# A two-layer diffusion block on one core: modulation sums, attention copies, layer 1's projection and its end rearranged

## The chip, the cores and the metric

The kernel runs on one core of one Trainium2 chip. The time is device microseconds of one execution; lower is better. Three runs gave 2876.41, 2872.47 and 2872.45 us, so the median is 2872.47 us.

## The reference

Two layers work on 1024 latent tokens and, in layer 0, on 256 context tokens, 1024 features each, in float32. Six modulation vectors per layer come from the conditions:

```python
m_lat = split(silu(c) @ ada_w[l] + ada_b[l], 6)      # m_ctx from c_ctx
h = x * (1 + m[1]) + m[0]
y = mixer(h)                                         # attention and output projection
x = layer_norm(DN_ALPHA * x + m[2] * y, ln_g[l, 0], ln_b[l, 0])
f = conv_ffn(x * (1 + m[4]) + m[3])                  # up, 3-tap convolution, silu(g) * a, down
x = layer_norm(DN_ALPHA * x + m[5] * f, ln_g[l, 1], ln_b[l, 1])
```

Layer 0's mixer has global attention (8 query heads over 2 key heads, "A") and neighbourhood attention (8 heads, "B"). Layer 1's has a window of 128 tokens to each side ("C"). All latent queries also read the context keys. Only the latent tokens of layer 1 are returned.

## The kernel before

Every large product is three fp32r products of operands split into a rounded part (hi) and the rest (lo). The hi cast is a ScalarE copy, the lo part a subtraction on VectorE or GpSimd. "The order by hand" below means that a region fixes the order of all engines' instructions; elsewhere only TensorE's order is fixed and a scheduler places the others.

**Layer 0's projection (`l0_project`).** `mm` banks of 128 tokens are made in turn with the weights `wq`, `wk`, `wv`, and then feature-wise with `wb` (the query part, `qB`) and `wb2` (the key part, `kB`), 12 evictions each. Beside it, the generator `ada_items` makes the modulation parts 2 to 5 of layer 0: eight chunks of 512 columns, each with four loads `araw` on SP's queue (512 KB), 16 multiply-adds `acc` on VectorE for the two conditions, and for each condition `ada_sum`: a hi/lo split `ahl`, two TensorE products with a matrix of ones into `small`, the bias row `abr`, and a store. `bg(n)` advances it by up to n steps and stops at a `"hold"`. What is left is drained when `kB` is done. The context rows are loaded by `load_x(2)` behind the four `wk` tokens that precede their first use; they wait for a buffer of the pool `xp`.

**Attention A (`groups_a`, `pv2_banks`).** Two key heads (kv), each with two context groups and eight latent groups. A latent group makes context scores, latent scores for two pairs of heads, the softmax, and ten banks of P transposes `T` in PSUM (three buffers), which `evict` copies to `PT`; the product `pv` reads these. `evict` takes VectorE in four of ten cases by a running counter, so the order of the engines within a group depends on where the counter stands.

**Output projection (`out_project`).** For each block of 128 tokens: load `yr`, split it into `yh`, `yl` (GpSimd makes `yl`), 48 products, gate, residual, statistics, normalisation. The block before is then turned by `finish`; in layer 1 this is `build_B1`, which also makes the four difference tiles `tt` of a Strassen-like scheme from block t and block t-4, t = 4 to 7. They go through memory (`T1`) and come back as T0 to T3 in `ffn7`; those of the last block stay in SBUF. Layer 1 takes the blocks in order 0 to 7. `first_x` and `rest` are the first products of layer 1's up projection.

**Layer 1's feed-forward (`ffn7`), in an order by hand.** First the up products and the convolution, with `store` and `mix` for the halves; then the down products in 77 steps of 12 matmuls into the banks `dx` and `dy`, with jobs hung on steps: loads of two steps ahead, `scale` of the residual, `evict` and `end`. `vs` holds a partial sum for the right half. The last nine steps run block by block, so that blocks 4 to 7 are done one after another, each followed by `evict` and `end`, where `finish_o` writes the output.

## Time and profile before

| what | value |
|---|---|
| median of three runs | 2872.47 us |
| profiled execution, its own time | 2874.48 us |
| its span | 2872.6 us |
| TensorE busy | 2747.7 us, 96% |
| VectorE / ScalarE / GpSimd busy | 2145.0 / 1388.0 / 667.2 us |
| chain that ended last | PE 70%, DVE 9%, issue 9%, DMA 5%, ACT 4%, POOL 2% |

PE is TensorE, PEld its weight loads, DVE VectorE, ACT ScalarE, POOL GpSimd, SP SyncE. In a timeline a row has start, duration, engine, line, operation, output and inputs, shape and count; in brackets stands the idle time of the engine before it and what ended it. In a table by windows the columns are the stretch, its length, busy time and count of PE, PEld, DVE, ACT and POOL, then the granted TensorE clock, the DMA share and GB/s.

### The profile page before, as it was taken

The numbers are of one execution on the slowest core, as the hardware profiler recorded it, in microseconds if no ns is written. First come the engines' busy times: TensorE is split into PE (matmuls) and PEld (weight loads), VectorE is DVE, ScalarE is ACT, GpSimd is POOL, SyncE is SP. The second block draws the span as 40 slices with busy tenths as digits, with TensorE's granted clock in tenths as the row PEclk, the third lists the DMA queues.
The fourth block names the chain that finished last, engine by engine and source line by source line (L and its number), as shares of the span: only waits on it lengthen the run. The fifth ranks groups of instructions, "written<-read, shape, count | busy, mean of one in ns | idle before, by whom it ended". The sixth has DMA issues, their size and how long they took to land.

```text
span 2872.6 us, 45400 instructions
## 1 busy us (share of the span) xinstructions
PE 2747.7 (96%) x16724; PEld 2244.9 (78%) x16724; DVE 2145.0 (75%) x3852; ACT 1388.0 (48%) x2607; POOL 667.2 (23%) x948
## 2 busy tenths in 40 slices
PE   8999799899999999999999999999998999999997
PEld 6787577777789988888888888766677788888886
DVE  4765676667588777888878656677778888888778
ACT  4321255567435655455553344167743555445541
POOL 4501243354451000000001002255644011111002
PEclk9999899999999999999999999999999999999998
DMA  7568611032558753333458525652244355555962
GB/s 272 153 206 279 214 32 43 9 134 92 169 161 243 216 165 108 110 114 110 121 197 294 173 98 171 199 165 81 83 132 162 120 180 176 165 173 205 329 218 90
DMA packets 369222, 457.02 MB, mean 159 GB/s; under 512 B 26008, under 2 KB 265016, under 8 KB 367464
## 3 DMA queue, kind: packets, MB, share of 16 engines
q1 hardware_dynamic: 341512, 369.53, 40.5%
q0 software_dynamic: 24592, 82.89, 8.3%
q8 instruction: 131, 2.15, 0.3%
q10 hardware_dynamic: 2896, 1.70, 0.2%
q14 instruction: 91, 0.75, 0.1%
HBM read 338.11 MB, written 115.93 MB: 158 GB/s over the span
## 4 chain that ended last, share of the span: by engine, by line
PE 70%; DVE 9%; issue 9%; DMA 5%; ACT 4%; POOL 2%; SPq 0%; ACTq 0%; POOLq 0%; DVEq 0%
PE q L1842 8%; PE x L1842 7%; PE y L1842 7%; PE S L882 4%; PE v L1842 4%; PE pv L1027 3%; PE mm L405 3%; PE mm L407 3%; PE mm L406 3%; PE T L1013 3%; PE dy L2524 3%; PE d L407 3%; PE d L406 3%; PE d L405 3%; PE dx L2524 2%
## 5 line engine op out<-in xcount | busy, mean ns | idle before, releaser
L906 POOL TENSOR_SCALAR P<-P,rin 128x640 f32<-128x640 f32 (+3 forms) x288 | 253.0, 882 | 333.8 <-DVE rin L905 301.8
L1816 DVE TENSOR_TENSOR w<-raw,w 128x512 fp32r<-128x512 f32 x308 | 208.6, 691 | 90.1 <-ACT w L1814 89.9
L113 DVE TENSOR_TENSOR w<-raw,w 128x512 fp32r<-128x512 f32 x315 | 204.5, 689 | 86.4 <-ACT w L112 83.1
L112 ACT CAST w<-raw 128x512 fp32r<-128x512 f32 x315 | 183.4, 620 | 173.4 <-PE d L407 67.2
L882 PE MATMUL S<-k,q 64*128 64x256 f32 (+2 forms) x1824 | 194.9, 337 | 17.3 <-DVE nm L2862 8.3
L903 ACT ACTIVATE P<-P,nm 128x641 f32<-128x641 f32 (+4 forms) x208 | 161.5, 778 | 84.9 <-DVE nm L2862 43.9
L1814 ACT CAST w<-raw 128x512 fp32r<-128x512 f32 x308 | 182.3, 620 | 15.1 <-DVE raw L1821 9.9
L882 PEld LDWEIGHTS S<-k,q 64*128 64x128 f32 x1824 | 136.9, 187 | 54.5 <-issue 19.1
L893 ACT COPY PT<-T 128x512 f32<-128x512 f32 (+1 forms) x250 | 134.9, 566 | 82.7 <-PE T L1013 80.0
L1027 PE MATMUL pv<-PT,v 128*64 128x128 f32 x2016 | 132.9, 279 | 16.6 <-ACT PT L893 13.9
L1013 PE MATMUL T<-ident,P 128*128 128x128 f32 x1008 | 135.8, 282 | 9.5 <-POOL P L906 3.3
L1027 PEld LDWEIGHTS pv<-PT,v 128*64 128x64 f32 x2016 | 108.5, 137 | 42.7 <-ACT PT L893 23.2
L405 PE MATMUL d<-w,w 128*128 128x512 f32 x352 | 137.5, 391 | 0.0
L407 PE MATMUL d<-w,w 128*128 128x512 f32 x352 | 137.0, 389 | 0.0
L406 PE MATMUL d<-w,w 128*128 128x512 f32 x352 | 137.0, 389 | 0.0
L1013 PEld LDWEIGHTS T<-ident,P 128*128 128x128 f32 x1008 | 110.4, 142 | 29.8 <-issue 17.4
L891 DVE COPY PT<-T 128x512 f32<-128x512 f32 (+1 forms) x166 | 110.4, 666 | 31.0 <-PE T L1013 21.1
L905 DVE RECIPROCAL rin<-den 128x1 f32<-128x1 f32 x288 | 46.0, 161 | 112.1 <-ACT P L903 108.7
L1842 PE MATMUL q<-T3h,w 128*128 128x512 f32 x352 | 121.1, 405 | 7.6 <-DVE ug L2479 4.0
L2524 PE MATMUL dy<-w,w 128*128 128x512 f32 x528 | 120.7, 390 | 0.0
L1842 PE MATMUL q<-T2h,w 128*128 128x512 f32 x352 | 115.9, 390 | 2.3 <-ACT q L2461 1.8
L903 ACT ACTIVATE P<-P,mc 128x1280 f32<-128x1280 f32 (+1 forms) x80 | 94.7, 1186 | 46.0 <-DVE mc L1148 41.6
(450 smaller groups left out, 7779.6 us busy)
## 6 DMA issues: line engine op xcount, KB each, us to landing
raw<-in_up_dram SPq DMA_DIRECT2D x132, 512.0 KB
raw<-in_down_dram SPq DMA_DIRECT2D x59, 512.0 KB
raw<-g SPq DMA_DIRECT2D x44, 512.0 KB
raw<-G SPq DMA_DIRECT2D x38, 512.0 KB
araw<-in_ada_w_dram SPq DMA_DIRECT2D x32, 512.0 KB
raw<-in_w_in_dram SPq DMA_DIRECT2D x28, 512.0 KB
g<-cv POOLq DMA_DIRECT2D x22, 512.0 KB, 3.0
G<-go POOLq DMA_DIRECT2D x44, 256.0 KB, 2.7
```

What stands on the lines that cost most here:

```text
L113: (lo_eng or nc.vector).tensor_sub(lo, s, f32(hi))
L405: nc.tensor.matmul(ps, lh, rh, start=first, stop=False)
L406: nc.tensor.matmul(ps, lh, rl, start=False, stop=False)
L407: nc.tensor.matmul(ps, ll, rh, start=False, stop=last)
L882: self.nc.tensor.matmul(outs[a], q[r, x, qs], k[r, y, ks], start=(i == 0), stop=(i == 2))
L903: nc.scalar.activation(P[:, :m], P[:, :m], AF.Exp, bias=negm, scale=-1.0, accum_out=den)
L906: nc.gpsimd.tensor_scalar(P[:, :n], P[:, :n], rin, 1.0, ALU.mult, ALU.mult)
L1013: nc.tensor.transpose(ps[:, s * 128 : (s + 1) * 128], P[a][:, cols[i + x] : cols[i + x] + 128], self.ident,)
L1027: nc.tensor.matmul(O[a * HD : (a + 1) * HD], v_of(a, vts[i + x]), pT[:, s * 128 : (s + 1) * 128], start=(i + x == 0), stop=(i + x == m - 1 ...
L1816: nc.vector.tensor_sub(half(i, 1), src[i], f32(half(i, 0)))
L1842: nc.tensor.matmul(ps, w[:, a, s], r[b][:, k], start=first and k + i == 0, stop=k == 3 and i == 2, skip_group_check=True,)
L2524: nc.tensor.matmul(banks[q][t], ga[i][:, a, c], wd[i][:, b], start=q < 2 and f + k == 0, stop=f == HF - 1 and k == 2, skip_group_check=True,)
```

## The change

1. Layer 0's projection. The context rows are loaded into the pool `raw` at the end of the first stage. The modulation is no longer advanced beside `wq` and `wk`. A sum's products stand in a list, `pend`, and are issued three visits or more after their split (or when the next chunk's first split comes); no hold ends a visit. `split`, `abr` and the bias loads are arranged per chunk.
2. Attention A. The ten `PT` copies of a latent group get named engines: `DDADA` and `AADDA` (D VectorE, A ScalarE).
3. Output projections. `yr` is loaded into `yl` and split in place.
4. Layer 1's end. Blocks in the order 0, 4, 1, 5, 2, 6, 3, 7; blocks 0 to 3 leave their float32 tiles as `b`, so `tt` takes four subtractions in place of six; the lo subtraction goes from GpSimd to VectorE; the last block's second half is scaled on VectorE; four weight parts move from `rest` to `first_x`; the Silu table is loaded in `rest`.
5. `ffn7`. One addition moves from `store` to `mix`; two more buffers in a new pool and one more in `fgs`, loads reach up to one pair further ahead; `vs` is gated and added to `z` in jobs of their own (`gated`, `shared`), so `evict` has three instructions and not four; `scale` earlier; the Sqrt table is loaded at step 67.
6. The last block's normalisation (`last_o`): Sqrt on ScalarE, a reciprocal, one Newton-like correction in five small ScalarE instructions, and the output in two halves on two queues.

The diff, cut:

```diff
@@ ada_items @@
-                        yield from self.ada_sum(tp, bank, acc[v], l, v, part, o, W)
-                yield
+                        if v == vecs[0]:
+                            while self.pend:
+                                self.pend.pop(0)[1]()
+                            br = self.t(tp, [64, W], "abr")
...
+                        self.ada_late(tp, bank, acc[v], br[i : i + 1], l, v, part, o, W, i)
+                        yield
@@ new: ada_late @@
+        hl = self.t(tp, [128, 2, W], "ahl", R, bufs=2)
+        nc.scalar.copy(hl[:, 0], acc)
+        nc.vector.tensor_sub(hl[:, 1], acc, f32(hl[:, 0]))
+        def late():
+            ps = bank()
+            nc.tensor.matmul(ps[:, :W], self.ones, hl[:, 0], start=True, stop=False)
+            nc.tensor.matmul(ps[:, :W], self.ones, hl[:, 1], start=False, stop=True)
+            nc.vector.tensor_add(br, ps[i : i + 1, :W], br)
+            nc.sync.dma_start(self.d["ada"][l, v, part : part + 1, o : o + W], br)
+        self.pend.append([0, late])
@@ l0_project @@
+            load_x(2)                      # behind split_k(1); before: ahead of wq's token 4
         def bg(n):
+            for x in self.pend:
+                x[0] += 1
+            if self.pend and self.pend[0][0] > 2:
+                self.pend.pop(0)[1]()
             for _ in range(n):
-                if next(ada[0], None) == "hold":
-                    break
+                next(ada[0], None)
-                if t > 7:                  # wq
-                    bg(2)
-                bg(1)                      # wk
-                bg(3)                      # wv
+                bg(1 if t < 2 else 2)
-                    bg(3)                  # qB, kB
                     n_ev.append(0)
+                    bg(0 if scale and len(n_ev) > 10 else 2 if n > 256 else 1)
@@ groups_a @@
+                        ("DDADA", "AADDA")[j] if t < NLAT else None,
@@ out_project @@
-                    yr = self.t(st, [128, 4, 128], "yr", bufs=2)
                     s = slice(4 * q, 4 * q + 4)
+                    yr = f32(yl[:, s])
@@ build_B1 @@
+                if t == NLAT - 1 and q == 1:
+                    nc.vector.tensor_scalar(s[:, j, :], ps[:, j, :], g, b, ALU.mult, ALU.add)
...
-            nc.gpsimd.tensor_sub(l, s, f32(h))
+            nc.vector.tensor_sub(l, s, f32(h))
...
-        nc.vector.tensor_sub(tt[0], b12, b11[0])
-        nc.vector.tensor_sub(tt[0], tt[0], b11[1])
+        nc.vector.tensor_sub(tt[0], b12, b11)
         nc.vector.tensor_sub(tt[1], b22, tt[0])
         nc.vector.tensor_sub(tt[2], b22, b12)
-        nc.vector.tensor_sub(tt[3], b21[0], tt[1])
-        nc.vector.tensor_add(tt[3], tt[3], b21[1])
+        nc.vector.tensor_sub(tt[3], b21, tt[1])
@@ ffn7 @@
+            def gated(t):
+                nc.vector.tensor_mul(vs[t], vs[t], gate[:, 512:])
+            def shared(t):
+                nc.vector.tensor_add(z[t][:, 512:], z[t][:, 512:], vs[t % 4])
...
-                job((20 + 3 * t) if t < 4 else (46 + 2 * (t - 4)), scale, t)
+                job(14 + 3 * t, scale, t)
+                job(37 + 2 * t, shared, t)
+                job(33 + t, gated, t)
+            job(6 * HF + 1, warm)
-                    n = i // 2 + min(5, 2 + i // 12)
+                    n = i // 2 + min(6, 2 + i // 10)
@@ l1_out @@
+                self.some_parts(E[0][1], [4, 3, 5, 6])      # first_x; before: rest
+                warm = self.t(st, [128, 1], "warm")         # rest
+                nc.scalar.activation(warm, self.mhalf[:, :1], AF.Silu)
-                io["w_out1"], d["yT1"], list(range(8)),
+                io["w_out1"], d["yT1"], [0, 4, 1, 5, 2, 6, 3, 7],
@@ new: last_o @@
+            nc.vector.bn_aggr(mv, s6.rearrange("p a b -> p (a b)"))
+            nc.scalar.activation(y, mv[:, 1:2], AF.Sqrt, bias=c[:, :1])
+            nc.vector.tensor_scalar(ve, mv[:, 1:2], LN_EPS, 1.0, ALU.add, ALU.mult)
+            nc.vector.reciprocal(y, y)
+            nc.vector.scalar_tensor_tensor(z, z, mv[:, 0:1], box["g"], ALU.subtract, ALU.mult)
...
+            for h, q in enumerate((nc.sync, nc.scalar)):
+                s = slice(h * 512, (h + 1) * 512)
+                nc.vector.scalar_tensor_tensor(
+                    z[:, s], z[:, s], rs, box["b"][:, s], ALU.mult, ALU.add
+                )
+                q.dma_start(io["out"][t * 128 : (t + 1) * 128, s], z[:, s])
```

## The prediction

> **What bounds the kernel now.** I read the page first, then a table by windows of 25 us over the whole span, then the timelines of the windows in which TensorE is not busy.

> ```profile
> span 2872.6 us, 45400 instructions
> PE 2747.7 (96%) x16724; PEld 2244.9 (78%) x16724; DVE 2145.0 (75%) x3852; ACT 1388.0 (48%) x2607; POOL 667.2 (23%) x948
> ```
> TensorE is busy 96% of the span, so only its 125 us of idle time and the time at a lower clock can be won. The windows say where these are:

> ```profile
> 75.00:100.00 25.00, 21.99 (x100) 17.57 (x99) 13.57 (x28) 8.86 (x20) 15.24 (x17) 0.93 0.14 41
> 125.00:150.00 25.00, 21.54 (x112) 17.93 (x111) 21.80 (x49) 8.53 (x23) 11.31 (x21) 0.93 0.75 225
> 175.00:200.00 25.00, 25.00 (x112) 20.62 (x111) 9.21 (x16) 7.37 (x13) 0.66 (x1) 1.00 0.40 126
> 325.00:350.00 25.00, 12.52 (x72) 8.51 (x71) 16.99 (x51) 7.82 (x22) 4.69 (x8) 0.66 0.53 181
> 2200.00:2225.00 25.00, 17.57 (x74) 13.94 (x73) 21.46 (x33) 10.86 (x21) 6.10 (x7) 0.94 0.65 215
> 2250.00:2275.00 25.00, 22.00 (x85) 17.64 (x84) 18.26 (x24) 11.22 (x18) 2.37 (x5) 0.86 0.31 98
> 2850.00:2872.60 22.60, 3.93 (x18) 2.92 (x16) 13.39 (x17) 0.00 (x0) 5.50 (x6) 0.65 0.23 91
> ```
> The first number behind the stretch's length is PE's busy time, "1.00" or less the granted clock. The windows of the up and down products (1100 to 1700, 2275 to 2600, 2650 to 2850 us) have 25.00 of 25 at 1.00: what the change does there to other engines is worth nothing while it stays covered. The six of them that are shown hold 48.0 us of the 125 (3.01 + 3.46 + 12.48 + 7.43 + 3.00 + 18.67) and most of the lost clock; attention holds much of the rest in small pieces. The row of 175 is shown as a full one: TensorE without idle, VectorE free for 16 of 25 us.

> **Context rows (part 1).**

> ```profile
> 78.13 0.43 PE L530 MATMUL tr<-ident,x 128*128 128x128 f32 x1 [3.01 <-DMA x<-in_ctx_dram]
> 105.95 2.67 ACT L112 CAST w<-raw 128x512 fp32r<-128x512 f32 x4
> 127.12 0.50 PE L321 MATMUL small<-ahl,ones 128*128 128x512 f32 x1 [1.75 <-DVE ahl L316]
> 135.27 0.47 PE L320 MATMUL small<-ahl,ones 128*128 128x512 f32 x1 [1.67 <-DVE abr L325]
> ```
> TensorE waits 3.01 us for the context rows. The window's clock of 0.93 adds 0.07 x 25 = 1.75 us. With the two DMAs (512 KB each) issued some 20 us sooner on SP, behind `split_k(1)`, both go: 3.0 to 4.8, I take 4.7. They now hold both buffers of `raw` until the last context turn, near 95 us, and what queues behind them is `wv`'s first load; its cast runs at 105.95 because it needs `wq`'s buffers first, so some 8 us are left for that load: nothing.

> **First sums (part 1).** Before, chunk 0 runs beside `wq` and `wk`, and its two sums stop TensorE for 1.75 and 1.67 us, with clock 0.93 again (1.75): 5.2 in all. After, chunk 0 starts with `wv` and a sum's products come three visits behind the split. In the trace the later sums, two visits behind, cost TensorE nothing until the drain. Chunk 0's multiply-adds move on VectorE to where the window of 175 shows room. Between 0 and 5.2, nearer the top since no row shows a later sum waiting: 4.0.

> **The drain at `kB`'s end (part 1).**

> ```profile
> 324.05 0.62 PE L882 MATMUL S<-k,q 64*128 64x256 f32 x6 [0.45 <-DVE qst L465]
> 331.51 4.71 DVE L228 SCALAR_TENSOR_TENSOR acc<-araw,cs,acc 128x512 f32<-128x512 f32 x7
> 336.33 0.79 PE L320 MATMUL small<-ahl,ones 128*128 128x512 f32 x1 [9.13 <-ACT ahl L315]
> 329.22 0.49 POOL L906 TENSOR_SCALAR P<-P,rin 128x256 f32<-128x256 f32 x1 [4.72 <-DVE rin L905]
> 344.59 0.80 PE L882 MATMUL S<-k,q 64*128 64x256 f32 x4
> ```
> Visits explain it. A chunk has 10 yields of which 4 are holds that end a visit, so at `bg(3)` it takes 6 visits; eight visits serve chunk 0 before `wv`, the 34 of `wv`, `qB` and `kB` serve 5.67 chunks. Chunk 7 is left whole: its multiply-adds block VectorE at 331.51, so the context groups' reciprocals are late, GpSimd normalises two tiles at 329 and the rest only after 336, and TensorE stands 9.13 us for a sum. From the first score (324.05) to block 0's (344.59) pass 20.5 us. After: 7 yields a chunk, 56 in all; visits allow 18 (`wv`: 1, 1, eight of 2), 17 (`qB`), 20 (`kB`) = 55. Only the last split and two sums are left, while chunk 7's last multiply-adds run beside the last two evictions. The context groups' own chain stays: the first tile is normalised 5.2 us after 324.05, eight take some 4 us more, and a rest of the sums lies between: block 0's scores at about 335, 9 us sooner. Ends: 5 (chunk 7 still late) and 16 (12.48 idle and the clock of 0.66). I take 9. The loads are as many as before in `qB`, four more each in `wv` and `kB`: 2 MB in 60 us or so, 35 GB/s, where the windows of 125 and 325 moved 225 and 181. Two `araw` buffers cover them; without that a late load holds SP's queue, behind which the `qst` stores of the evictions stand, and TensorE would wait for `mm`.

> **`PT` copies (part 2).**

> ```profile
> 369.41 2.78 PE pv L1027 x48
> 458.18 2.77 PE pv L1027 x48
> 497.52 2.77 PE pv L1027 x48
> 591.69 2.77 PE pv L1027 x48
> 369.41:458.18 88.77, 85.90 (x941) 69.19 (x942) 63.53 (x192) 51.53 (x85) 32.19 (x25) 1.00 0.09 28
> 497.52:591.69 94.17, 84.18 (x940) 68.69 (x940) 58.94 (x174) 52.15 (x86) 32.13 (x25) 1.00 0.05 15
> 535.40 1.09 PE L1027 MATMUL pv<-PT,v 128*64 128x128 f32 x16 [1.42 <-ACT PT L893]
> 534.79 1.05 ACT L893 COPY PT<-T 128x512 f32<-128x512 f32 x2
> 402.16 0.69 DVE L891 COPY PT<-T 128x512 f32<-128x512 f32 x1 [0.15 <-PE T L1013]
> 408.17 1.23 DVE L1143 TENSOR_SCALAR_CACHE_REDUCE P<-S 128x1024 f32<-128x1024 f32 x1 [0.92 <-PE S L882]
> ```
> In the chain of waits a group's 48 `pv` mark its period. Six groups of the first key head take 88.77 us, 14.80 each, 14.32 of it busy; six of the second 94.17, 15.70 each, 14.03 busy. The work is the same; only the counter's phase differs (`DAADA` twice, then `ADAAD` twice). In the second, bank 0 of the first half goes to ScalarE, which is in two exponentials, and copies only at 534.79; TensorE waits 1.42 us. In the first, VectorE copies bank 0 at 402.16, ahead of need. After, VectorE has banks 0 and 1 there, and in the second half ScalarE, idle then, has 0 and 1 while VectorE is in its 1.23 us reductions. That is the first head's order and better, for both heads. VectorE gets one copy more per group (0.69 us of 14.8; it is busy 63.53 of 88.77). Ends: all idle gone, 8 x 0.48 + 8 x 1.67 = 17.2; or an order as bad as the second head's for both, a loss of 8 x 0.9 = 7.2. If both come to the first's period the gain is 8 x 0.9 = 7.2, with half of what is left 12. I take 10.

> **Layer 1's end (part 4).**

> ```profile
> 2202.22 1.80 DVE L1771 TENSOR_TENSOR yl<-hst,hst 128x512 f32<-128x512 f32 x1
> 2201.80 1.68 POOL L1746 TENSOR_TENSOR h3lbl<-hst,h3lbh 128x512 fp32r<-128x512 f32 x1 [2.70 <-DVE h3lbh L1745]
> 2205.26 0.68 DVE L1446 TENSOR_TENSOR hst<-o,gate 128x512 f32<-128x512 f32 x1
> 2209.38 1.06 PE L1728 MATMUL tr<-ident,x 128*128 128x128 f32 x8 [2.87 <-issue]
> 2218.12 1.21 DVE L1872 TENSOR_TENSOR T0l<-gk,T0h 128x1024 fp32r<-128x1024 f32 x1
> 2221.19 0.50 PE L1842 MATMUL v<-T0l,w 128*128 128x512 f32 x1 [4.55 <-DVE T0l L1872]
> 2253.40 0.79 PE L1842 MATMUL q<-T3h,w 128*128 128x512 f32 x1 [3.00 <-DVE ug L2479]
> 2248.03 1.28 ACT L2349 ACT_TABLE_LOAD   x1 [2.41 <-DVE cv L2321]
> ```
> The last product before `first_x` ends near 2200.4; its gate waits on VectorE until 2205.26, behind block 6's differences. That gives the stalls of 2.87 and 4.55 us. Block 3 in its place needs two casts and two lo parts there, none over 0.68, where block 6 has seven instructions, among them the one of 1.80: the gate comes near 2201 and the turn follows `first_x`, 26 products of 0.23, with no stall, ending near 2207.3. Then for block 7, each of 512 columns at 0.68 as the gate's row: half the scaling on VectorE, half on ScalarE (some 1.5 us), a cast and a lo part (1.1), four subtractions (2.7), T0's lo (1.21 + 2 x 0.68 = 2.6; its other blocks have come back long before). T0 is ready near 2215.2 and not 2221.2, 6.0 us. The parts moved to `first_x` are seven such instructions, 4.8 us, of a VectorE that waits for statistics there. The third stall (3.00) has the table load of 1.28 in it; that goes to `rest`, where ScalarE waits for VectorE's differences. The clocks of 0.94 and 0.86 lost 1.5 and 3.5. 6.0 + 1.3 + half of 5.0 = 9.8, I take 10. Top 15 (7.4 + 3 + 5); 3 if only the first stall goes. Between, blocks 4 to 6 put their differences behind earlier products, 3.8 us of VectorE in a block of 11.8: covered, and if not, the products wait for the bank `o`.

> The subtraction of 1.80 us began while GpSimd had its lo part (2201.80 to 2203.48) and ended 0.54 us behind it, so I take its length for a wait on GpSimd, which the change removes. [...]

> **`yr` (part 3)** saves a buffer; a block's load now waits until `yl` is read two blocks back, 11.8 us ahead of need: nothing. **Up products (part 5)**: VectorE moves, under full TensorE: nothing.

> **The tail (parts 5, 6).**

> ```profile
> 2823.85 30.08 PE L2524 MATMUL dy<-w,w 128*128 128x512 f32 x132
> 2832.28 0.67 DVE L2536 TENSOR_TENSOR tt<-v,dx 128x512 f32<-128x512 f32 x1
> 2860.23 0.68 DVE L2534 TENSOR_TENSOR tt<-dy,gate 128x512 f32<-128x512 f32 x1
> 2865.95 0.33 SPq L3093 DMA_DIRECT2D out_dram<-z  x1
> ```
> TensorE ends at 2853.93, but block 7's gate starts at 2860.23, 6.3 us behind, since VectorE works off a queue; the output row's last DMA starts near 2866.0 and the span ends 6.6 later. Eight additions of 0.67 (L2536) leave the queue, 5.4 us, and the last loads' casts come a pair sooner. `last_o` itself I take as long as the old chain, 5.7 from gate to DMA: GpSimd's part becomes small instructions on ScalarE beside the 1.3 us subtraction. Ends 0 (`gated` and `shared`, 12 instructions, fill the queue again) and 7.2 (all of the lag, and a last DMA of half the size); nearer the top, since those 12 come 30 steps earlier: 6.5.

> **Sum.** 4.7 + 4.0 + 9 + 10 + 10 + 6.5 = 44.2 us; 2872.6 - 44.2 = 2828.4. The profiled execution took 2874.48 with its 2872.6 of span; the median, 2872.47, is at the span, so I take 2828 for the time.

> **Rivals.** (1) The stalls move: chunk 7's sums still hold the first groups (5), T0 remains late on VectorE (4), `PT` gives 4, the tail 3, the sums 2, the rows 4.7: 22.7, that is 2850. For it: every stall here sits beside a busy VectorE. Against: the work ahead of each is really less. (2) Slower, by the copies alone: banks 2 and 3 of the second half are both VectorE's, and if the scheduler puts them behind the reductions of 1.23 us, three `T` banks fill and TensorE stands. At 2.5 us a group the 16 groups lose 40 against today, while the others give 34: 2878. It decides from 2.1 us a group. Against: the worst order in the trace costs 0.9. (3) The stalls go but the low clock stays, having another cause. The sum holds 1.75 + 0.5 + 2.5 and some 2 at the drain for the clock, 6.8 in all, so 2835. [...] The windows of 0.93 with no other stall in them speak against it.

> **Chances.** Forecast 0.60 (its own range 2815 to 2842), better than that 0.08, rival 3 0.10, rival 1 0.18, rival 2 0.04. Low end 2808: the tops of all terms sum to 65.4. High end 2852, just past rival 1. One measurement tells 0.2%, 5.7 us, from no change: of rival 1 some 0.03 may reach that far, so faster 0.93, within 0.03, slower 0.04.

> **What would show it.** No wait for `x<-in_ctx_dram`; windows 75 and 125 at clock 1.00; no `acc` rows of VectorE behind the first attention score beyond a few us, block 0's scores near 11 us after the first; equal periods of both heads, 14.2 to 14.6 us; T0's first product some 14 us after the output projection's last; block 7's gate right at TensorE's end. Wrong if `PT` or `T` waits grow on TensorE, if `araw` loads stop `qB` or `wb2`, or if new stalls appear in the down products.

## The result, and the profile after

Four executions took 2826.76, 2831.16, 2832.47 and 2836.89 us: a median of 2831.81 us beside 2872.78 for the kernel before, a ratio of 0.985 (0.984 to 0.987). Measured once more, beside two of the experiments, the medians were 2832.89 and 2871.73 (0.987, 0.985 to 0.989). The forecast of 2828 us lies 4 us under that, the range holds it. The profiled execution below is the fastest of the four, 2826.76 us with a span of 2825.0; against the span before it is 47.6 us shorter, where the medians differ by 39 to 41. Where those 7 us come from is part of what follows.

The page of the kernel after, its span and first row of engines:

```profile
span 2825.0 us, 45395 instructions
PE 2739.5 (97%) x16724; PEld 2244.3 (79%) x16724; DVE 2155.0 (76%) x3887; ACT 1380.8 (49%) x2596; POOL 641.9 (23%) x933
```

Its windows of 25 us, at the places where the kernel before lost time (PE's busy time behind the length, the clock behind POOL):

```profile
75.00:100.00 25.00, 25.00 (x122) 20.29 (x120) 16.74 (x32) 9.09 (x21) 18.84 (x22) 1.00 0.26 78
125.00:150.00 25.00, 25.00 (x116) 20.50 (x115) 19.47 (x38) 7.17 (x19) 5.63 (x6) 1.00 0.82 254
225.00:250.00 25.00, 22.78 (x119) 16.13 (x118) 17.70 (x29) 3.20 (x6) 1.05 (x2) 0.86 0.82 282
325.00:350.00 25.00, 21.85 (x198) 16.77 (x199) 16.61 (x47) 12.01 (x19) 10.18 (x11) 0.94 0.64 222
850.00:875.00 25.00, 20.71 (x132) 18.63 (x131) 20.53 (x39) 15.98 (x35) 3.02 (x3) 0.86 1.08 316
2200.00:2225.00 25.00, 22.51 (x98) 17.70 (x97) 21.22 (x31) 11.31 (x18) 1.08 (x2) 1.00 0.22 64
2800.00:2825.00 25.00, 14.73 (x66) 11.86 (x64) 16.68 (x23) 1.86 (x6) 4.75 (x6) 0.90 0.22 84
```

75 and 125 are full at 1.00; 325 has 21.85 of 25 where it had 12.52, 2200 has 22.51 at 1.00 where it had 17.57 at 0.94. Two windows are worse: 225 (22.78, clock 0.86; 25.00 at 1.00 before) and 850 (20.71, 0.86; the same products had 22.49 at 1.00 before, from 875 to 900 us). TensorE's timeline of the kernel after at these places:

```profile
232.82 0.76 PE L330 MATMUL small<-ahl,ones 128*128 128x512 f32 x1 [2.22 <-DVE abr L332]
317.06 0.62 PE L910 MATMUL S<-k,q 64*128 64x256 f32 x6 [0.50 <-DVE qst L489]
322.99 0.47 PE L330 MATMUL small<-ahl,ones 128*128 128x512 f32 x1 [3.15 <-DVE rin L935]
324.80 1.94 PE L1043 MATMUL T<-ident,P 128*128 128x128 f32 x8 [1.10 <-POOL P L936]
326.67 1.61 PE L910 MATMUL S<-k,q 64*128 64x256 f32 x12
855.86 0.79 PE L429 MATMUL d<-w,gT 128*128 128x512 f32 x1 [4.29 <-ACT w L112]
2190.28 0.50 PE L1860 MATMUL v<-T0l,w 128*128 128x512 f32 x1 [1.01 <-DVE T0l L1890]
2219.40 0.50 PE L1860 MATMUL q<-T3h,w 128*128 128x512 f32 x1 [1.71 <-DVE ug L2498]
```

From the first score (317.06) to block 0's scores (326.67) pass 9.6 us and not 20.5; T0's first lo product waits 1.01 us and not 4.55, the product behind the third stall 1.71 and not 3.00. In the chain of waits the second key head's groups have this period:

```profile
477.30 2.77 PE pv L1057 x48
...
548.64 2.77 PE pv L1057 x48
```

Five groups in 71.34 us, 14.27 each (15.70 before). Counted at the same matmul of both traces, the kernel after is ahead by:

| at | before, us | after, us | ahead, us |
|---|---|---|---|
| projection, behind the context rows' wait | 81.13 | 76.57 | 4.6 |
| last tokens of `wv` | 200.13 | 189.37 | 10.8 (10.3 without two sum products of 0.23) |
| first score | 324.05 | 317.06 | 7.0 |
| block 0's scores | 344.59 | 326.67 | 17.9 |
| second key head's first score | 470.32 | 451.59 | 18.7 |
| attention B | 604.93 | 575.38 | 29.6 |
| layer 0's output projection, first product | 753.33 | 723.61 | 29.7 |
| the up products behind the first context `d` | 884.25 | 861.07 | 23.2 |
| layer 1's output projection, last product | 2200.22 | 2175.97 | 24.3 |
| T0's first lo product | 2221.19 | 2190.28 | 30.9 |
| first down product | 2674.25 | 2635.05 | 39.2 |
| last down product's end | 2853.93 | 2814.74 | 39.2 |
| span's end | 2872.59 | 2824.98 | 47.6 |

So there are two losses, 3.3 us (from 10.3 down to 7.0) between `wv` and the first score and 6.5 us in the output projection. In this pair of traces every other term gives about what was forecast or more. It is one execution of each kernel, though: four traces below hold the kernel before's layer 0 projection and reach the first score at 318.4 to 324.1 us, six hold the kernel after's and reach it at 314.1 to 317.1, so a row of this table can be some microseconds off by the execution alone.

### The profile page after: what moved, and what is told of

It is laid out like the page before. It is cut to its first block, busy times and chain, and to the rows that moved or that the text cites. A ratio compares the mean times of both kernels' runs of the same rounds, so it can differ in the third digit from the quotient of the medians.

```text
span 2825.0 us, 45395 instructions
## 1 busy us (share of the span) xinstructions
PE 2739.5 (97%) x16724; PEld 2244.3 (79%) x16724; DVE 2155.0 (76%) x3887; ACT 1380.8 (49%) x2596; POOL 641.9 (23%) x933
## 4 chain that ended last, share of the span: by engine, by line
PE 74%; issue 9%; DVE 7%; DMA 3%; ACT 3%; POOL 2%; SPq 0%; ACTq 0%; DVEq 0%; POOLq 0%
PE q L1860 8%; PE x L1860 8%; PE y L1860 8%; PE S L910 4%; PE v L1860 4%; PE dy L2544 4%; PE mm L429 4%; PE mm L431 4%; PE mm L430 4%; PE T L1043 3%; PE pv L1057 3%; PE dx L2544 3%; PE d L431 3%; PE d L429 3%; PE d L430 3%
## 5 line engine op out<-in xcount | busy, mean ns | idle before, releaser
L112 ACT CAST w<-raw 128x512 fp32r<-128x512 f32 x315 | 183.3, 620 | 163.9 <-PE d L431 67.1
L1832 ACT CAST w<-raw 128x512 fp32r<-128x512 f32 x308 | 182.2, 620 | 17.2 <-DVE raw L1839 7.5
L429 PE MATMUL d<-w,w 128*128 128x512 f32 x352 | 137.5, 391 | 0.0
L1057 PE MATMUL pv<-PT,v 128*64 128x128 f32 x2016 | 131.0, 278 | 4.6 <-ACT PT L923 2.4
L2544 PEld LDWEIGHTS dy<-w,w 128*128 128x128 f32 x528 | 98.9, 188 | 21.6 <-DVE w L113 0.6
L1860 PE MATMUL v<-T0h,w 128*128 128x512 f32 x352 | 115.5, 389 | 0.0
```

The costliest lines, as they stand in the source:

```text
L429: nc.tensor.matmul(ps, lh, rh, start=first, stop=False)
L1057: nc.tensor.matmul(O[a * HD : (a + 1) * HD], v_of(a, vts[i + x]), pT[:, s * 128 : (s + 1) * 128], start=(i + x == 0), stop=(i + x == m - 1 ...
L1860: nc.tensor.matmul(ps, w[:, a, s], r[b][:, k], start=first and k + i == 0, stop=k == 3 and i == 2, skip_group_check=True,)
L2544: nc.tensor.matmul(banks[q][t], ga[i][:, a, c], wd[i][:, b], start=q < 2 and f + k == 0, stop=f == HF - 1 and k == 2, skip_group_check=True,)
```

## The experiments

Each median is set against the kernel before measured beside it (2871.7 to 2874.2 us). The intervals of the ratios reach 3 to 6 us to each side. The variants e1, e4, e7 and e10 have intervals that overlap the kernel after's, and so has e12 with e11: their times alone don't tell them apart, and what is concluded there rests on the rows of the traces. e8, e11 and e12 lie clear of the kernel after.

### The parts alone

Four kernels are the kernel before with one part of the change each. Layer 0's projection alone, the hunks of `ada_items`, `ada_late`, `load_x`, `bg` and its calls:

> The kernel before with nothing but the change of layer 0's projection (context rows, sums behind their splits, visits). Theory A, by the trace after: rows 4.5, first sums 5.5, a new stall of 2.2 at a sum beside `qB` with its half clock for minus 5, the old one of 2.1 at 263 gone for 2, first score to block 0's scores 9.6 instead of 20.5 for 10.9: 18 us, so 2855. Rival B: attention's first groups give part of the drain's gain back, since VectorE and GpSimd had work left that the drain covered: under 13 us, 2860 or more.

Measured (e5): 2857.52 beside 2873.63, 16.1 us less (ratio 0.994, 0.993 to 0.996): between the two theories, nearer to A, whose rows the trace has (a stall of 2.32 us at a sum near 234, 9.6 us from the first score to block 0's scores). The named engines alone:

```diff
+                        ("DDADA", "AADDA")[j] if t < NLAT else None,
```

> The kernel before with nothing but the named engines for the PT copies. Theory A: the copies' order alone makes the periods of the latent groups 14.3 us in both key heads, TensorE without a wait, apart from two groups of the first head where the modulation's columns are made (16 us); nearly all of the gain is in the second head: 0.8 + 10.8 = 11.6 us, so 2861. Rival B: the gain in the trace after comes partly from groups that start in another phase because the drain ahead of them is shorter; then the names alone give under 6 us, 2867 or more.

Measured (e2): 2867.14 beside 2873.19, 6.1 us less (0.998, 0.997 to 0.999). The trace has theory A's periods, 14.27 us in the second head and two groups of 16.1 in the first, and wins 11.8 us from block 0's scores to attention B. But then it is 3.4 us slower up to the up products, as much as two steps at half clock take (at 635 and 741 us), where the kernel before has none; and it has two stalls of 1.7 and 2.0 us in layer 1's up products that the kernel before has not. So the mechanism is A's, and what reaches the end is at B's bound; why the two late stalls came is open. Layer 1's end alone:

> The kernel before with nothing but the change at layer 1's end (order of blocks, `b` tiles, lo parts on VectorE, half of the last scaling on VectorE, four weight parts and the table load moved) and, in layer 1 alone, the split in place that makes room for it. Theory A: it stands alone: T0's first lo product 14 to 15 us after the output projection's last product, the stalls of 2.87 and 4.55 gone but for 1.0, the third 1.7 instead of 3.0, clock 1.00 in all of it: 12.8 us, so 2860. Rival B: part of that was given by the earlier parts (another phase of the evictions of the last blocks): under 9 us, 2864 or more.

Measured (e3): 2862.97 beside 2873.19, 10.2 us less (0.996, 0.995 to 0.997). The time lies between the two theories; the row is A's: T0 follows the last output product by 14.30 us (20.97 before), as in the kernel after. The feed-forward of layer 1 alone:

> The kernel before with nothing but the changes in layer 1's feed-forward: `mix`, the two pools, `gated` and `shared`, the earlier `scale`, `last_o`. Theory A: from TensorE's end to the span's end 10.2 us instead of 18.7 (8.4), and some 2 us from the up products, where `mix` and not `store` has the addition: 10 us, so 2863. Rival B: the up products' part came from layer 1's end: 8 us, 2865.

Measured (e6): 2863.34 beside 2873.63, 10.3 us less (0.995, 0.994 to 0.997). TensorE's end to the span's end is 9.4 us (18.7 before). From T0 to the first down product it takes 447.2 us and not 453.1; some 3 of these 5.9 are half clock (1.7 lost and not 4.7), nearly all the rest comes in a dozen steps of 0.2 to 0.5 us at `q` products. Since layer 1's end is as before here, the up products' part is this edit's: theory A.

The four sum to 42.7 us, the whole change gives 39 to 41. The parts add up within their intervals; what is left over has the sign of part 3, which is next, but is too small to be told from nothing.

### Part 3: the split in place

```diff
-                    yr = f32(yl[:, s])
+                    yr = self.t(st, [128, 4, 128], "yr", bufs=2) if len(order) > 8 else f32(yl[:, s])
```

> The kernel after, with the buffer `yr` back in layer 0's output projection (layer 1 keeps the split in place). Theory A: the split in place shifted GpSimd's two subtractions `yl<-yl,yh` so that they lie over VectorE's residual row; the row `x<-x,hst` that starts at 806.52 takes 3.56 us, until GpSimd is done at 809.52, and a block takes 12.8 us where it took 11.8, which makes VectorE the bound of this stage and costs 5 to 6 us up to the first context down product. Then the long row falls under 2 us, the block period goes back to 11.8, the wait of 4.29 us at the first `d` falls to about 2, and the time falls by 5 us. Rival B: VectorE is late there because attention ends sooner and its own work is as much as before, or because the loads come late; then the long row stays, the wait at `d` stays above 4, and the time is within 1.5 us of the kernel after.

What the expectation starts from, in the timelines of VectorE and GpSimd of the kernel after:

```profile
793.73 3.60 DVE L1478 SCALAR_TENSOR_TENSOR x<-x,hst 128x512 f32<-128x512 f32 x1
806.52 3.56 DVE L1478 SCALAR_TENSOR_TENSOR x<-x,hst 128x512 f32<-128x512 f32 x1
811.44 0.69 DVE L1478 SCALAR_TENSOR_TENSOR x<-x,hst 128x512 f32<-128x512 f32 x1
806.18 0.80 POOL L1746 DMA_DIRECT2D T<-tt  x1 [0.93 <-DVE tt L1745]
807.00 2.52 POOL L1458 TENSOR_TENSOR yl<-yl,yh 128x512 fp32r<-128x512 f32 x2
```

and of this experiment (e1), with TensorE's first `d`:

```profile
800.65 1.51 DVE L1478 SCALAR_TENSOR_TENSOR x<-x,hst 128x512 f32<-128x512 f32 x1
812.42 1.52 DVE L1478 SCALAR_TENSOR_TENSOR x<-x,hst 128x512 f32<-128x512 f32 x1
812.11 2.98 POOL L1458 TENSOR_TENSOR yl<-yr,yh 128x512 fp32r<-128x512 f32 x2 [2.42 <-ACT yh L1457]
856.22 0.49 PE L429 MATMUL d<-w,gT 128*128 128x512 f32 x1 [2.25 <-ACT w L112]
```

In the kernel after the row of 512 columns ends 0.56 us behind GpSimd's second subtraction, 3.56 us after its start, where the same row of the block's other half, with GpSimd out of the way, takes 0.69; the blocks follow each other in 12.79 us. With `yr` back the row takes 1.52, since it still ends 0.55 us behind the first of the two subtractions; the blocks take 11.77, the wait at `d` is 2.25 and not 4.29. The long row had begun 0.48 us before the first subtraction, while GpSimd issued a DMA (806.18), and so it is in all five blocks. Neither alone holds it: in e1 the row at 809.23 begins 0.34 us into such an issue and takes 0.69, and in the kernel after two such rows from 722.97 on take 1.28 together though a subtraction begins at 723.70, and it is GpSimd's pair that is longer (2.94 us for 2.52). Why the two together do stays open. From the output projection's first product to the up products behind the first `d` the trace takes 131.0 us and not 137.5. Over all traces this stretch is 136.8 to 139.1 us in the five with the split in place and 130.6 to 133.6 in the nine without. Of the 6.4 us 3.5 are idle time and 2.4 half clock behind the wait at `d`. The median is 2828.1, 3.7 to 4.8 us less, within overlapping intervals. Theory A holds, by the rows.

### The two slow groups of the first key head

In the kernel after two groups of the first head take 16.1 us (17.7 in its second trace, with half clock behind both stalls). The timelines of TensorE, VectorE and GpSimd there:

```profile
387.71 1.67 PE L910 MATMUL S<-k,q 64*128 64x512 f32 x11 [1.71 <-DVE P L1156]
384.97 1.30 DVE L370 TENSOR_TENSOR m1ab<-m1ab,m1c 128x8 f32<-128x8 f32 x2
384.85 1.34 POOL L936 TENSOR_SCALAR P<-P,rin 128x1280 f32<-128x1280 f32 x1 [0.25 <-DVE m1s L367]
```

Two operations of 8 columns (0.16 us each before them) took 1.30 us, and ended 0.08 us behind GpSimd's normalisation; the context reductions `P` stand behind them on VectorE, and TensorE waits 1.71 us for these.

On top of the edit of e1:

```diff
-                nc.vector.tensor_mul(ab[:, 0], ct[:, 0:8], s1)
+                nc.gpsimd.tensor_mul(ab[:, 0], ct[:, 0:8], s1)      # and the three beside it
```

> The kernel of e1_yr_back with the four small operations that make the modulation's columns (`m1s`, `m1ab`) on GpSimd and not VectorE. Theory A: in two groups of the first key head these stood on VectorE behind GpSimd's normalisations (two rows of 8 columns each took 1.30 us and not 0.3), the context reductions came late and TensorE waited 1.71 and 1.75 us; on GpSimd they wait for nothing, the two groups take 14.3 to 14.8 us and not 16.1, and the time falls by 3 us and by up to 3 more where the clock had fallen with them: 2825 to 2822. Rival B: GpSimd's own normalisation of the second pair comes later by their 1 to 2 us, and the transposes wait for P: no gain, 2828 to 2830.

Measured (e8): 2817.55 beside 2873.63 (0.980, 0.979 to 0.982). The chain of waits of this kernel, first head:

```profile
350.64 2.77 PE pv L1057 x48
...
421.98 2.77 PE pv L1057 x48
```

Five groups in 71.34 us, 14.27 each, no slow one left; theory A, though the time fell by more than its 3 to 6 us. Beside e11, below, this is the fastest kernel: 14 to 15 us under the kernel after, where the idle time that went is 85.0 - 78.0 = 7.0 us and half clock 4.1. To e1 the traces differ by 6.5 us (6.9 in the first key head) and the medians by 10.6; TensorE's instructions stand in the same order in both, and the 4 us between are not assigned.

### The stall beside `qB`

SyncE's and VectorE's timelines of the kernel after:

```profile
223.22 0.43 SPq L219 DMA_DIRECT2D araw<-in_ada_w_dram  x1
230.74 0.75 DVE L228 SCALAR_TENSOR_TENSOR acc<-araw,cs,acc 128x512 f32<-128x512 f32 x1 [2.86 <-DMA araw<-in_ada_w_dram]
232.01 0.67 DVE L332 TENSOR_TENSOR abr<-small,abr 1x512 f32<-1x512 f32 x1
```

Its window from 190 to 240 us (the two numbers behind the clock are the DMA share and GB/s):

```profile
190.00:240.00 50.00, 47.78 (x259) 36.63 (x259) 36.22 (x59) 8.32 (x16) 4.37 (x8) 0.93 0.93 289
```

The load issued at 223.22 is there at 230.74; VectorE waits 2.86 us for it, the bias row stands behind it, and the product of 232.82 behind that. The length of this stall is not the kernel's own. In its second trace the same product waits 0.73 us and the clock stays:

```profile
231.78 0.47 PE L330 MATMUL small<-ahl,ones 128*128 128x512 f32 x1 [0.73 <-DVE abr L332]
```

In the five other traces with this code it waits 1.22 to 2.32 us. The experiments below were planned on the first trace's 2.22.

```diff
             for t in range(4, NT):
                 tok(t, wk, 256, ev_kva)
+                if t > 5:
+                    bg(1)
...
-                    bg(0 if scale and len(n_ev) > 10 else 2 if n > 256 else 1)
+                    bg(0 if scale and len(n_ev) > 10 else 2 if n > 256 and not (scale and len(n_ev) < 6) else 1)
```

> The kernel after, with four steps of the modulation advanced beside the last four `wk` tokens and four steps fewer beside `qB`. Theory A: the stall of 2.22 us at 232.82 and the half clock behind it come from loads: between 190 and 240 us the DMA engines are 0.87 to 1.00 busy, a load of `araw` issued at 223.22 lands only at 230.74, VectorE stands behind it, and the bias row of the first sum, on which the next sum's bank waits, comes behind that. With four loads moved to 150 to 180 us, where the share is 0.14 to 0.49, the stall goes or falls under 0.7 us and the time by 4 to 5 us. Rival B: loads are late all the same since the evictions' stores hold the queue: the stall moves to another sum and the time stays within 1.5 us. Rival C: the first sums beside `wv` stop TensorE again as in the kernel before (1.75 and 1.67 us), and it gets slower by 2 to 5 us.

Measured (e4): 2837.61 beside 2873.19 (0.987, 0.986 to 0.989), 5 us above the kernel after, with overlapping intervals. The stall at 232 is gone and the trace 4 us ahead behind it; then the weights of `wb2` come 1.49 us late, and beside `wv` TensorE idles 1.2 us more. At the product that the kernel after has at 257 us it is 2.0 ahead of that kernel's first trace and 1.1 behind its second, so no gain is shown. What made the trace slower came later, in stages with the same code, as 3 us of idle time (88.0 and not 85.0) and 4.5 of half clock: none of the three theories in numbers, and C's sign for another reason.

```diff
-            banks[0] = e3.enter_context(self.pool("paf", bufs=1, space=PSUM))
+            banks[0] = e3.enter_context(self.pool("paf", bufs=2, space=PSUM))
```

> The kernel of e8_yr_hook with two PSUM buffers and not one for the sums beside `qB` and `kB`, so that a sum's products no longer wait until VectorE, late behind a load of `araw`, has added the bias of the sum before. Theory A: that wait is the whole of the stall of some 2.1 us near 232: it goes, and the time falls by 2 to 4 us, to 2814 to 2815. Rival B: TensorE then waits for a bank of the projection instead, since the same VectorE queue evicts these: within 1 us of 2817.5.

Measured (e11): 2817.49 beside 2871.73 (0.981, 0.979 to 0.983): no difference to e8, as B has it, but not for B's reason, since TensorE waits for no bank of the projection. Its timeline of TensorE and its window:

```profile
253.32 0.79 PE L429 MATMUL mm<-hh,w 128*128 128x512 f32 x1 [3.08 <-ACT w L112]
```
```profile
225.00:250.00 25.00, 25.00 (x153) 18.95 (x151) 20.15 (x34) 4.75 (x9) 3.23 (x7) 1.00 0.93 311
```

The stall at the sum is gone, and one of 3.08 us has come at the cast of `wb2`'s first weights, with the DMA engines 0.93 busy in the 25 us ahead. The last kernel has both edits:

> The kernel of e11_yr_hook_banks with the four steps of the modulation moved from `qB` to the last four `wk` tokens, as in e4_spread. There the trace showed the next stall of the same supply: TensorE waits 3.08 us for the cast of the first `wb2` weights, whose loads stand among those of `araw` at a DMA share of 0.93. Theory A: only the order of the loads is at fault; with four of them in 150 to 180 us (share 0.2 to 0.5) neither the sums nor the weights are late, TensorE's idle time falls from 75.0 to about 72 us and the time to 2814 or less. Rival B: from 190 to 275 us the transfers themselves are the limit (0.92 to 0.99 busy in e4_spread too): a stall of 1 to 2 us stays at the weights, and the sums beside `wv` cost 1 us as they did there: within 2 us of 2817.5.

Measured (e12): 2821.84 beside 2874.21 (0.982, 0.980 to 0.983), 4 us more than e11, with overlapping intervals; its idle time rose by 3.6 us and did not fall. TensorE's timeline has two waits for weights:

```profile
252.72 0.50 PE L429 MATMUL mm<-hh,w 128*128 128x512 f32 x1 [2.56 <-ACT w L112]
257.78 0.80 PE L429 MATMUL mm<-hh,w 128*128 128x512 f32 x1 [2.02 <-ACT w L112]
```

Theory A is out. Rival B's mechanism fits, its "within 2 us" does not: in e4, e11 and e12 the stall goes from one consumer of the loads to the next, and the DMA engines are 0.85 to 0.99 busy from 190 to 275 us. That the transfers themselves are the limit is argued and not shown, since no run moved fewer bytes there.

### Layer 1's end taken apart

The lo parts back on GpSimd:

```diff
-            nc.vector.tensor_sub(l, s, f32(h))
+            nc.gpsimd.tensor_sub(l, s, f32(h))
```

> The kernel after with the lo parts of layer 1's turned blocks back on GpSimd. Theory A, a VectorE instruction with two SBUF operands stands while GpSimd is in an instruction that began first: the subtraction `hst,hst` behind the second lo part takes about 1.8 us again and not 0.69, and so does another one of the block; VectorE has 1.4 us less of its own per block and 1 to 2 us more of standing, block 7's gate and T0 come 0.5 to 2 us later, and the time rises by up to 2 us. Rival B: the length came from the operands: rows of 0.69 throughout, VectorE free 1.4 us sooner per block, T0 not later, the time the same or lower by 1 us.

The subtraction `hst,hst` of block 7 in the kernel after, and in this experiment (e7) with GpSimd's lo part and T0's product:

```profile
2186.60 0.68 DVE L1795 TENSOR_TENSOR w<-hst,hst 128x512 f32<-128x512 f32 x1
```
```profile
2194.11 1.80 DVE L1795 TENSOR_TENSOR w<-hst,hst 128x512 f32<-128x512 f32 x1
2193.69 1.68 POOL L1778 TENSOR_TENSOR h3lbl<-hst,h3lbh 128x512 fp32r<-128x512 f32 x1 [2.67 <-DVE h3lbh L1777]
2198.91 0.50 PE L1860 MATMUL v<-T0l,w 128*128 128x512 f32 x1 [1.79 <-DVE T0l L1890]
```

1.80 us again in place of 0.68, ending 0.54 behind GpSimd; T0 follows the last output product by 15.58 us and not 14.30. Theory A holds in the rows. The median (e7), 2838.32 beside 2873.63 (0.988, 0.986 to 0.989), is 5 to 6 us above the kernel after, with overlapping intervals. The idle time is 87.2 us (85.0 and 84.4 in the two traces of the kernel after), so 2 to 3 us are the kernel's own, T0's 1.3 among them; half clock has 20.9.

The old order of the blocks (the difference tiles are then all made with block 3's tiles, so the output is another; the work and its timing are the same):

```diff
-                io["w_out1"], d["yT1"], [0, 4, 1, 5, 2, 6, 3, 7],
+                io["w_out1"], d["yT1"], list(range(8)),
```

> The kernel after with layer 1's output projection in the order 0 to 7. Theory A: the order is what brings the last gate forward, since block 6 with its four differences and lo parts stands in front of block 7's gate and not block 3 with its two casts and two lo parts: a stall of 1 to 3 us comes back at the last block's transposes and T0 comes 2 to 3 us later: 2.5 to 5 us slower with the clock. Rival B: it is the shorter list (four differences and not six, no lo part on GpSimd) that did it: the stretch from the last output product to T0's first lo product stays at 14.3 us within 1 us, and the time within 1.5.

Measured (e10): 2834.17 beside 2871.73 (0.987, 0.985 to 0.989), 1.3 us over the kernel after beside it. TensorE's timeline:

```profile
2188.84 0.66 PE L1759 MATMUL tr<-ident,x 128*128 128x128 f32 x4 [1.16 <-DVE x L400]
2197.54 0.50 PE L1860 MATMUL v<-T0l,w 128*128 128x512 f32 x1 [1.61 <-DVE T0l L1890]
```

The stall at the last transposes is back (1.16 us), T0's wait 1.61, and T0 follows the last output product by 16.83 us: 2.5 of the 6.7 us are the order's. The other 4.2 are the rest of part 4's, the lo parts' 1.3 from the experiment above among them; the four subtractions, the scaling on VectorE and the moved weight parts were not taken apart. Theory A is right in what it names, B in the time.

### The clock

```diff
(no edit: the kernel after once more)
```

> The kernel after once more, beside the two below on the same chip, as their reference. Theory A: TensorE's idle time is the kernel's own (85 us in its first trace), while the time lost at half clock depends on where each stall falls and differs from execution to execution (10.8 to 24.2 us in the traces so far): idle again 85 within 2 us, the loss to half clock anywhere between 10 and 25, a median of 2829 to 2836. Rival B: both are the kernel's own: the trace repeats the half-clock stretches behind the same stalls (at 232, 325, 570, 854, 1052, 1840 us).

Measured (e9): 2832.89 us. From the traces' rows, TensorE's idle time and the time lost at half clock (half of its busy time in the stretches recorded at 0.50). Span less busy time by the pages gives 0.5 to 0.7 us more idle time in each row.

| kernel | span, us | idle | lost at half clock | rest |
|---|---|---|---|---|
| before | 2872.6 | 124.2 | 20.3 | 2728.1 |
| after | 2825.0 | 85.0 | 14.9 | 2725.1 |
| after, once more | 2829.6 | 84.4 | 19.2 | 2725.9 |
| e1, `yr` back | 2822.3 | 80.7 | 15.9 | 2725.7 |
| e8, and columns on GpSimd | 2815.8 | 78.0 | 10.8 | 2726.9 |
| e11, and two banks | 2811.4 | 75.0 | 9.2 | 2727.1 |

Theory A: in the two traces of one kernel the idle time as a whole repeats within 0.6 us, the loss at half clock does not. It explains 4.3 us of the 4.6 by which the two traces differ; the second trace's execution took 2831.37 us, close to the median, so most of what the first one promised beyond the median is that.

## Why the prediction was right, and where not

The sum was 44.2 us, the trace has 47.6, the medians 39 to 41. Term by term, by the table of matmuls:

- **Context rows**, 4.7: 4.6. No wait for `x<-in_ctx_dram` is left.
- **First sums**, 4.0: 5.7 by the last tokens of `wv` (10.3 less 4.6). The half clock behind the sum at 135 us, 1.7 of it, stands in this trace of the kernel before alone and in none of the three others with its code.
- **The loads**, nothing: minus 3.3 by the first score, 5.2 lost at the new stall and 2 won where this trace of the kernel before had one near 263 us. The step that failed is "2 MB in 60 us or so, 35 GB/s", with "Two `araw` buffers cover them". It counted the chunk that was added and not all that moves: from 190 to 240 us the DMA engines are 0.93 busy, and the load of 512 KB issued at 223.22 takes 7.5 us. That `araw` loads stop `qB` was among the prediction's own signs of being wrong, and it came; the hazard was named with the wrong victim: not `mm`, but the bank of the next sum.
- **Drain**, 9: 10.9. Block 0's scores come 9.6 us after the first, 11 were forecast.
- **`PT` copies**, 10: 11.6, but 0.8 in the first head and 10.8 in the second. The forecast of equal periods holds (14.27) except for the two groups with the modulation's columns, which went from 15.0 to 16.1 us, in e2 too, where the names are the only edit: VectorE, fuller by one copy, has no room left for what waits there. With the half clock behind these two the first head loses more often than it wins: 124.7 to 130.5 us in seven traces with the names, 124.9 to 127.0 in four without.
- **`yr`**, nothing: minus 6.5 in the trace, 4 to 5 in the medians. The prediction looked at when the load can start and not at when GpSimd would then subtract: over VectorE's residual row. That is the step that cost most. The two losses make 9.8 us; that the forecast still came within 4 us of the median is luck, since layer 1's end, the tail and the drain were sized too low by nearly as much. With those as forecast the sum would have been 34.4 and the time 2838, inside the range all the same.
- **Layer 1's end**, 10: 15.0 from the last output product to the first down product, up products among them. T0 alone is 6.7 (6.0 forecast), the rest the third stall (1.3), the half clock behind it and behind T0's, all gone (some 4.4), and 2.7 that the forecast of "nothing" for the up products missed. There TensorE waited 0.2 to 0.5 us at each of a dozen `q` products. In both traces the rows there, of 0.39 us, start 0.23 apart, so most of such a wait is hidden by the row before it, and the windows read 25.00 of 25, but for two that the prediction counted as full (24.97 and 24.77). The prediction took the 1.80 us of the subtraction for a wait on GpSimd, and e7 bears that out: 0.68 us without, 1.80 with GpSimd's lo part.
- **Tail**, 6.5: 8.4, above the upper end of 7.2. VectorE's timeline, and the two queues of the output:

```profile
2814.77 0.69 DVE L2559 TENSOR_TENSOR tt<-dy,gate 128x512 f32<-128x512 f32 x1 [0.41 <-PE dy L2544]
2820.23 0.33 SPq L3138 DMA_DIRECT2D out_dram<-z  x1
2820.90 0.39 ACTq L3138 DMA_DIRECT2D out_dram<-z  x1
```

The gate comes 0.04 us behind TensorE's end (2814.74); the lag of 6.3 is all gone, and from the last DMA's start the span ends after 4.1 us and not 6.6, of which the prediction had 0.9 in its upper end alone.

Summed: 44.2 - 0.1 + 1.7 - 3.3 + 1.9 + 1.6 - 6.5 + 5.0 + 1.9, and 1.2 between (0.2 in attention B, 1.1 from the up products to layer 1's output projection): 47.6.

That is what one trace of each kernel adds up to. By the means over the traces that hold the same code of a stage the context rows give 3.8, the first sums 4.0, the loads minus 3.1, the drain 10.7, the first head minus 1.7 and the second 10.4, `yr` minus 6.4, layer 1's end 14.4, the tail 9.1 and the stretches between 1.8. They sum to 43 us, nearer to the medians; the first key head and the first sums make most of the difference.

**The rivals.** Stalls that move (1): two did, for 10 us, and not those it named. `PT` copies slower (2): no; apart from the two with the modulation's columns the groups of both heads take 14.27 us. The clock (3): the loss fell from 20.3 to 14.9 in the first pair of traces, 5.4 of the 6.8 that the sum held, but to 19.2 in the other one. So it was right that the gain from the clock is not safe. That the low clock had a cause other than the stalls is not shown: stalls of 1.71 us (e1) and 2.22 (the kernel after) were followed by half clock, as the last section has it.

## What to carry to other kernels

A buffer saved by working in place moves the instruction that fills it; ask which other engine's instruction it will then lie beside, above all between VectorE and GpSimd (here 3.56 us for 0.69). Before work is packed into a shorter stretch, add up all its transfers there, not those added. And when two versions differ by a few microseconds, compare TensorE's idle time and its time at half clock apart: in the two traces of one kernel here the first repeated (85.0 and 84.4 us), the second did not (14.9 and 19.2). A term read from one trace of each kernel holds the luck of both, so look at the same stage in every trace that has the same code.

## What the runs showed of the hardware

```profile
386.14:389.55 3.41, 1.84 (x15) 1.29 (x17) 2.47 (x12) 0.10 (x1) 0.05 (x1) 1.00 0.00 0
389.55:392.96 3.41, 3.41 (x38) 2.90 (x36) 3.28 (x8) 1.88 (x3) 0.00 (x0) 1.00 0.02 5
```

and in e1:

```profile
387.39:390.80 3.41, 1.70 (x14) 1.07 (x13) 2.49 (x12) 0.33 (x1) 0.28 (x1) 1.00 0.00 0
390.80:394.21 3.41, 3.41 (x24) 3.08 (x24) 2.42 (x6) 0.32 (x1) 0.00 (x0) 0.50 0.02 5
```

In the first the stall is cut by the grid (1.84 of 3.41 busy) and the clock stays; in the second it lies in one step (1.70 busy) and the next 3.41 us run at half. Over fourteen traces and some 11,350 steps recorded at full clock, each of the 75 with TensorE busy under 0.4 of the step was followed by half clock, none of those over 0.63 was, and of the 177 between, the two above among them, 49 were; in the kernel after alone 5 of 5, none of 792 and 2 of 13. So a stall of some 2 us cost 0, 1.7 or 3.4 us beside its length.

Three kinds of VectorE rows stood behind GpSimd: a residual row of 512 columns (3.56 us for 0.69 in the kernel after, ending 0.56 behind GpSimd), a subtraction (1.80 in e7 for 0.68 in the kernel after, 0.54 behind), and rows of 8 columns in the kernel after (1.30 us for two, 0.16 each before, 0.08 behind).
